# Seven block products in the down projection of an encoder layer's feed-forward part

## The chip, the cores and the metric

One core of one Trainium2 chip runs one launch of the kernel. The time is device microseconds. TensorE (PE) multiplies and writes to PSUM banks of 128 x 512 fp32; VectorE (DVE), ScalarE (ACT) and GpSimd (POOL) work on tiles; SyncE (SP) issues the loads, in order.

## What is computed

One layer of an encoder over 256 rows of width 2048, all in fp32:

```python
h = x + rms_norm(mixed, g_mix_post)          # mixed: attention and recurrence, through w_out
fn = rms_norm(h, g_ffn_pre)
ff = (silu(fn @ w_ffn_gate) * (fn @ w_ffn_up)) @ w_ffn_down   # 2048 -> 5632 -> 2048
h = h + rms_norm(ff, g_ffn_post)
gate = sigmoid(rms_norm(h, g_ple_pre) @ w_ple_gate)
ple = p @ w_ple_proj                          # the embedding, 256 -> 2048
h = h + rms_norm(gate * ple, g_ple_post)
```

## The kernel before

**Products.** Rows are two blocks (t) of 128, contraction blocks (k) are of 128, and columns come in chunks (c) of 512. Each fp32 factor is split into a high part that the fast format holds and a low part; a product of blocks is three matmuls (high x high, high x low, low x high; L521 to L523 in a plain product, L530 to L532 in a seven-product unit). A weight tile holds two contraction blocks by 512 columns, 512 KB: SP loads it into `wr` (L432), ACT casts it into `wh` (L457), DVE subtracts to make `wl` (L482). Some buffers are lent from tiles not needed meanwhile (`lent_w`, `lent_r`, `lent_t`).

**Seven products.** In the gate/up stage a `Group` computes two chunks at once (one of gate, one of up). For a pair of contraction blocks, two row blocks and two chunks, a plain unit (`p`) makes 8 block products, 24 matmuls; an `s` unit makes 7 products in Strassen's manner (`seven`), 21 matmuls. An `s` unit needs sums of weight blocks, two more tiles that DVE makes with four 512-wide operations (L502, L506) and that are cast and split as the others, and sums of the left-hand blocks (`act_sums`). It uses eight banks: four `c` sums that every unit adds to, and four `p` sums that `Seven`-type code in `early` combines (one ACT copy, four DVE additions) once the last `s` unit is through; `late` then adds them to the `c` sums. The two rings of four banks swap roles from group to group (`flip`). The kinds of a gate/up group:

```python
FIRST = "ppppspsp"
KINDS = "ppspspsp"
```

**Stages of the feed-forward part.** The 5632 columns are 11 gate/up groups, in parts of 4, 4 and 3. After each part the down projection adds that part's share: for each of four chunks in turn, `seg` runs 8 (part 2: 6) plain pairs into two banks `acc`, and `down_post` copies them to `mg` on ACT (part 0) or adds them to it on DVE (part 1); in part 2 `sub_post` adds them, squares them on ACT and multiplies by the gain. The last gate/up group of a part is finished inside the down stage: six late operations (L1506, L1513), two transposes of four matmuls (L309), and the split of the result into `mid0h` and `mid0l` (L289, L291).

**Order.** Every engine takes its queue in order. The order across engines is set while the program is written: a planner keeps a clock for each engine, with a cost for each kind of instruction, and picks, of the tasks that are ready, the one that would start first; a task may be given an advance or a delay (`late`).

**The embedding.** Its first half (chunks 0 and 1, tile `ple0`, 1 MB) is made ahead of the feed-forward part and kept on the chip until the last stage; the second half is made after the down projection from the same split `pTh`, `pTl` of p. As the gate/up stage begins, `lend_h` saves h to DRAM (L1328) and lends its space to weight tiles; `give_back` reloads it in part 2 (L1348).

Of the kernel before, what the change touches and what calls it, by code (L numbers as in the profile page):

```python
# [61 lines left out]
LANDED = 2.5  # L62
FIRST = "ppppspsp"
# [164 lines left out]
def layer(ctx: ExitStack, tc: tile.TileContext, a: dict, out: bass.AP):  # L228
# [140 lines left out]
    class Group:  # L369


        def __init__(self, w, n0, lhs, ks, kinds, post):
            self.lhs, self.post, self.banks, self.i0 = lhs, post, {}, len(tiles)
            self.early = Event()
            self.units = list(zip(ks, kinds))
            self.early = Event()
            for (k, _), kind in self.units:
                i = len(tiles)
                tiles.extend((w[c], k, n0[c]) for c in range(2))
                by_dma.update({"d": (i, i + 1), "e": (i + 1,), "c": (i,)}.get(kind, ()))  # L380
                if kind == "s":
                    singles[i + 1] = 1
                    for n in range(2):
                        sums[i + 2 + n] = (i, n)
                        tiles.append(None)
            segs.append(self)
# [174 lines left out]
    def run_group(g, flip):  # L561
        rings = ("sm", "acc") if flip else ("acc", "sm")
# [596 lines left out]
    def open_p2():  # L1159
# [7 lines left out]
        t2["ple", 0] = rs.tile([P, NT, DA], F32, name="ple0")  # L1167
# [4 lines left out]
        t2["pTh"] = rs.tile([P, 2, S], F32R, name="pTh")  # L1172
        t2["pTl"] = rs.tile([P, 2, S], F32R, name="pTl")
        t2["pw"] = rs.tile([P, NT, N], F32, tag="mid", name="pw", bufs=2)[:, 0, :]
        t2["pw"] = t2["pw"].rearrange("p (k s) -> p k s", k=2)
# [10 lines left out]
    pT = Act(2)  # L1186
# [10 lines left out]
    def load_p2():  # L1197
        yield from load_gain("g_mix_post")
        done(ev_gain["mix"])
        yield dma(256)  # L1200
        here = Event()
        nc.sync.dma_start(t2["pw"], a["pT"].rearrange("(k p) s -> p k s", p=P))
        done(here)
# [3 lines left out]
        done(ev_h)  # L1207
        yield here
        yield from split(t2["pTh"], t2["pTl"], t2["pw"], 2 * S)
        pT.blocks(t2["pTh"], t2["pTl"], 0, 2)  # L1210
        pT.pair(0)

    class Sub:
# [10 lines left out]
        def chunk(self, c, ch, add=False):  # L1224
# [29 lines left out]
            if early:  # L1254
                yield ev_gain[self.name]
                for t in range(NT):
# [3 lines left out]
                    )  # L1260
            done(self.chunks[c])
# [11 lines left out]
    def next_norm(sub, nxt, rstd, ev_rstd, g_next):  # L1273
# [21 lines left out]
        for c in range(4):  # L1295
            if c > 1:
                yield nxt.ev[4 * c - 8]
            for b in range(2):
# [7 lines left out]
                plan.add(transpose_h(4 * c + 2 * b, hi, lo, nxt, sub.gname), plan.now)  # L1306
# [31 lines left out]
    def lend_gain():  # L1338
        t = t2["pool"].tile([P, 2, 2, N], F32, tag="gain", name="lent_t")
        lend("ts", [t[:, n, :, :] for n in range(2)])  # L1340

# [83 lines left out]
    def ple_post(c):  # L1425
        def post(ch):
# [3 lines left out]
            release(ch)  # L1430
        return post

    def embedding(c):
        seg(Chunk(ple_post(c)), "w_ple_proj", c * N, pT, [(0, 0)])
# [6 lines left out]
    def sub_post(sub, c, add=False, after=None):  # L1441
        def post(ch):
            if c == 3:
                plan.add(after(), plan.now)
# [3 lines left out]
    def after_mix():  # L1448
# [5 lines left out]
        Chunk(sub_post(mix, c, after=after_mix), None if c else open_p2) for c in range(4)  # L1454
# [16 lines left out]
    class Gated:  # L1471


        def __init__(self, mid, kk0):
            self.mid, self.kk0 = mid, kk0
# [20 lines left out]

        def late(self, g):
# [4 lines left out]
            for t, n, x in (  # L1502
                (0, "c11", e[:, 0, :]), (1, "c21", e[:, 1, :]), (0, "c12", u[0]), (1, "c22", u[1]),
            ):
# [3 lines left out]
                if n[2] == "1":  # L1508
# [29 lines left out]
    class Mid(Act):  # L1538
        def __init__(self, name):
            super().__init__()  # L1540
            self.name, self.halves = name, {}

        def tiles(self, i):
            if i not in self.halves:
                t = (big(2 * i, f"{self.name}h{i}"), big(2 * i + 1, f"{self.name}l{i}"))
                self.halves[i] = t
                self.blocks(*t, 8 * i, 8)
            return self.halves[i]

    def down_post(part, c):  # L1550
        def post(ch):
            sl = slice(c * N, (c + 1) * N)
            mg = t2["mg"]
            for t in range(NT):
                if part == 0:
                    yield act(N)
                    nc.scalar.copy(mg[:, t, sl], ch.accs[t])
                else:
                    yield dve(N)
                    nc.vector.tensor_tensor(  # L1560
                        out=mg[:, t, sl], in0=ch.accs[t], in1=mg[:, t, sl], op=ALU.add
                    )
            release(ch)
        return post
# [7 lines left out]
    for part, (f0, f1) in enumerate(parts):  # L1572
# [5 lines left out]
        for c in range(4):  # L1578
            last = part == len(parts) - 1
            post = sub_post(ffn, c, True, after_ffn) if last else down_post(part, c)  # L1580
            seg(Chunk(post), "w_ffn_down", c * N, mid,
                [(f0 * 4 + k, k) for k in range(0, (f1 - f0) * 4, 2)],
                after=(lambda: load_sqrt()) if last and c == 3 else None)
# [183 lines left out]
```

## Time and profile before

| | |
|---|---|
| median of 3 runs | 1179.17 us (1179.09 to 1180.56) |
| profiled execution: time, span | 1181.19 us, 1179.4 us |
| granted TensorE clock | 0.997 |
| busy: PE, DVE, ACT | 1159.9, 878.8, 686.9 us |
| moved by DMA | 236.43 MB, 200 GB/s |

Times in the profile count from the span's first instruction. A row of a group or of the timeline names line, engine, operation, output<-inputs and shapes; in square brackets stands the idle time of the engine ahead of it and what ended it. The gate/up stage runs from about 361 us, with the down stages of parts 0, 1 and 2 at 534.7 to 622.6, 791.4 to 879.3 and 1006.4 to 1072.6 us.

### The profile page before, as it was taken

To read this page: it belongs to the slowest core of one execution; us is meant where nothing else is said; L and a number is where in the kernel's file an instruction comes from. 1 tells how busy PE (TensorE), PEld (TensorE's weight loads), DVE (VectorE), ACT (ScalarE), POOL (GpSimd) and SP (SyncE) were. 2 spreads that over 40 slices of the span, in tenths; PEclk is the share of its full clock that TensorE was granted. 3 is DMA by queue.
4 is the path that set the end of the run, shared out by engine and by line. 5 is a ranking of instruction groups with operands and counts; after the bars stand their busy time and mean duration, and the time that the engine had idled before them with its cause. 6 is when DMAs were issued, how large, how long until landed. Compare 5 with 4: busy or idle time off the path is not lost.

```text
span 1179.4 us, 14527 instructions
## 1 busy us (share of the span) xinstructions
PE 1159.9 (98%) x5292; PEld 959.8 (81%) x5292; DVE 878.8 (75%) x1118; ACT 686.9 (58%) x925; POOL 1.6 (0%) x13
## 2 busy tenths in 40 slices
PE   7999999999999999999999999999999999999996
PEld 5888888888888888888888888888888888888885
DVE  5567868778649898897456899895466988757663
ACT  6687777766548565465445556554335556456652
POOL 0000000000000000000000000000000000000000
PEclk9999999999999999999999999999999999999998
DMA  8855566545963755677665575576656557764851
GB/s 302 286 164 189 168 194 194 163 159 168 327 214 114 289 197 179 213 232 247 191 195 164 164 235 175 177 255 213 195 163 195 167 178 249 270 190 146 259 167 71
DMA packets 69783, 236.43 MB, mean 200 GB/s; under 512 B 7504, under 2 KB 13520, under 8 KB 68560
## 3 DMA queue, kind: packets, MB, share of 16 engines
q1 hardware_dynamic: 69568, 235.44, 61.7%
q8 instruction: 41, 0.67, 0.2%
q14 instruction: 30, 0.25, 0.1%
q10 hardware_dynamic: 144, 0.08, 0.0%
HBM read 231.29 MB, written 4.19 MB: 200 GB/s over the span
## 4 chain that ended last, share of the span: by engine, by line
PE 87%; DVE 6%; DMA 3%; ACT 2%; issue 1%; SPq 1%; DVEq 0%; ACTq 0%
PE acc L523 17%; PE acc L522 17%; PE acc L521 17%; PE c L521 7%; PE c L522 7%; PE c L523 7%; DVE wl L482 2%; PE p L531 2%; PE p L532 2%; PE p L530 2%; PE c L530 2%; PE c L532 2%; PE c L531 2%; PE tr L309 2%; DMA av<-in_w_rg_i 1%
## 5 line engine op out<-in xcount | busy, mean ns | idle before, releaser
L482 DVE TENSOR_TENSOR wl<-wr,wh 128x1024 fp32r<-128x1024 f32 (+1 forms) x322 | 375.9, 1182 | 145.0 <-ACT wh L457 144.3
L457 ACT CAST wh<-wr 128x1024 fp32r<-128x1024 f32 (+1 forms) x322 | 323.5, 1020 | 221.8 <-PE acc L523 135.3
L521 PE MATMUL c<-wh,hT_mix_hi 128*128 128x512 f32 x400 | 157.3, 393 | 0.0
L523 PE MATMUL c<-wh,hT_mix_lo 128*128 128x512 f32 x400 | 155.8, 390 | 0.0
L522 PE MATMUL c<-wl,hT_mix_hi 128*128 128x512 f32 x400 | 155.8, 389 | 0.0
L521 PE MATMUL acc<-wh,hT_hi 128*128 128x512 f32 x320 | 129.0, 403 | 6.5 <-ACT wh L457 6.4
L522 PE MATMUL acc<-wl,hT_hi 128*128 128x512 f32 x320 | 126.7, 396 | 1.7 <-DVE wl L482 1.7
L523 PE MATMUL acc<-wh,hT_lo 128*128 128x512 f32 x320 | 126.6, 396 | 0.0
L457 ACT CAST wh<-lent_t 128x1024 fp32r<-128x1024 f32 x56 | 58.6, 1052 | 56.6 <-DVE lent_t L506 36.7
L523 PEld LDWEIGHTS c<-wh,hT_mix_lo 128*128 128x128 f32 x400 | 75.1, 188 | 16.0 <-DVE hT_mix_lo L297 0.2
L521 PEld LDWEIGHTS c<-wh,hT_mix_hi 128*128 128x128 f32 x400 | 75.1, 188 | 15.1
L522 PEld LDWEIGHTS c<-wl,hT_mix_hi 128*128 128x128 f32 x400 | 75.2, 188 | 15.0
L482 DVE TENSOR_TENSOR wl<-lent_r,wh 128x1024 fp32r<-128x1024 f32 (+1 forms) x58 | 64.4, 1118 | 22.2 <-ACT wh L457 22.1
L457 ACT CAST wh<-lent_r 128x1024 fp32r<-128x1024 f32 (+1 forms) x58 | 55.4, 969 | 41.7 <-PE acc L523 25.0
L521 PEld LDWEIGHTS acc<-wh,hT_hi 128*128 128x128 f32 x320 | 61.2, 191 | 18.9 <-ACT wh L457 7.2
L482 DVE TENSOR_TENSOR wl<-lent_t,wh 128x1024 fp32r<-128x1024 f32 x56 | 66.9, 1218 | 10.6 <-ACT wh L457 10.5
L522 PEld LDWEIGHTS acc<-wl,hT_hi 128*128 128x128 f32 x320 | 61.1, 191 | 14.6 <-DVE wl L482 2.9
L523 PEld LDWEIGHTS acc<-wh,hT_lo 128*128 128x128 f32 x320 | 61.1, 191 | 13.0
L521 PE MATMUL acc<-wh,hT_ffn_hi 128*128 128x512 f32 x112 | 44.0, 393 | 0.0
L521 PE MATMUL acc<-wh,mid0h 128*128 128x512 f32 x112 | 43.8, 391 | 0.0
L521 PE MATMUL acc<-wh,mid1h 128*128 128x512 f32 x112 | 43.8, 391 | 0.0
L523 PE MATMUL acc<-wh,hT_ffn_lo 128*128 128x512 f32 x112 | 43.7, 390 | 0.0
(324 smaller groups left out, 2239.6 us busy)
## 6 DMA issues: line engine op xcount, KB each, us to landing
wr<-in_w_in SPq DMA_DIRECT2D x79, 512.0 KB, 4.3
wr<-in_w_ffn_down SPq DMA_DIRECT2D x68, 512.0 KB, 4.3
wr<-in_w_ffn_gate SPq DMA_DIRECT2D x60, 512.0 KB, 4.2
wr<-in_w_ffn_up SPq DMA_DIRECT2D x60, 512.0 KB, 4.6
wr<-in_w_out SPq DMA_DIRECT2D x32, 512.0 KB, 4.5
wr<-in_w_ple_gate SPq DMA_DIRECT2D x32, 512.0 KB, 4.4
lent_r<-in_w_ffn_gate SPq DMA_DIRECT2D x28, 512.0 KB, 3.9
lent_r<-in_w_ffn_up SPq DMA_DIRECT2D x28, 512.0 KB, 4.4
```

The lines of the kernel that those rows point to most:

```text
L309: nc.tensor.transpose(tr[:, b, t * P : (t + 1) * P], src, ident)
L457: nc.scalar.copy(his[i][:, j, :], raws[i][:, j, :])
L482: nc.vector.tensor_tensor(out=los[i][:, j, :], in0=raws[i][:, j, :], in1=f32(his[i][:, j, :]), op=ALU.subtract,)
L521: nc.tensor.matmul(accs[t], hi[:, sl], wh[:, j, :], start=st, stop=False)
L522: nc.tensor.matmul(accs[t], hi[:, sl], wl[:, j, :], start=False, stop=False)
L523: nc.tensor.matmul(accs[t], lo[:, sl], wh[:, j, :], start=False, stop=sp)
L530: nc.tensor.matmul(o, lh, wh, start=start, stop=False)
L531: nc.tensor.matmul(o, lh, wl, start=False, stop=False)
L532: nc.tensor.matmul(o, ll, wh, start=False, stop=stop)
```

## The change

The down projection works in groups of two chunks with `s` units: in parts 0 and 1 two groups with two and three of them; in part 2 one group with one, and chunks 2 and 3 plain as before. `Down` takes the place of `down_post`: its `early` is that of the gate/up groups (now in a base class `Seven`), its `late` adds the combined sums to `mg`. `mid_sums` makes the block sums of `mid` in two tiles, for which it uses the space of `ple0` and of the split p. So the first half of the embedding is written to DRAM once made (`kept_ple`) and read back in part 2, when p is loaded and split a second time (`ple_back`). The squares, the transposes and the final additions of the last chunk of a sub-layer get an advance of 2 us in the planner (`URGENT`).

```diff
+DOWN = {
+    4: ("p2 p6 p10 p8 s0 p12 s4 p14", "p2 p6 s0 p10 s4 p12 s8 p14"),
+    3: ("p2 p6 p10 s0 p4 p8", ""),
+}
+URGENT = -2.0
...
     def run_group(g, flip):
+        if g.after:
+            g.after()
...
-                plan.add(self.squares(c, t, src, squared[t]), plan.now)
+                plan.add(self.squares(c, t, src, squared[t]), plan.now, URGENT if c == 3 else 0.0)
...
-                plan.add(transpose_h(4 * c + 2 * b, hi, lo, nxt, sub.gname), plan.now)
+                plan.add(transpose_h(4 * c + 2 * b, hi, lo, nxt, sub.gname), plan.now, URGENT)
...
+    def ple_back():
+        yield from load_pT(pTs[1])
+        t2["ple", 0] = t2["pool"].tile([P, NT, DA], F32, tag="ple0", name="ple0")
+        yield dma(1024)
+        nc.sync.dma_start(t2["ple", 0], t2["kept", "ple"])
+
+    def mid_sums(mid, ks):
+        rs = t2["pool"]
+        a_ = rs.tile([P, 2, 2, 4, P], F32R, tag="ple0", name="sums_a")
+        b_ = rs.tile([P, 2, 4, P], F32R, tag="pT", name="sums_b")
...
+        for k, (hi, lo) in zip(ks, at_):
+            mid.sums[k] = hi, lo
+            yield mid.ev[k]
+            yield mid.ev[k + 1]
+            yield dve(2 * S, take="uv")
+            v = at.tile([P, 2, NT, P], F32, tag="at0_hi", name="v")
+            nc.vector.tensor_tensor(
+                out=v.rearrange("p k t m -> p k (t m)"), in0=f32(mid.pair_of(k, 0)),
+                in1=f32(mid.pair_of(k, 1)), op=ALU.add,
+            )
+            yield from act_sums(mid, k, v)
...
             release(ch)
+            if c == 1:
+                t2["kept", "ple"] = kept.tile([P, NT, DA], F32, name="kept_ple")
+                yield dma(1024)
+                nc.sync.dma_start(t2["kept", "ple"], t2["ple", 0])
...
+    class Down(Seven):
...
+        def late(self, g):
+            yield g.early
+            mg, c0 = t2["mg"], self.c0
+            for t, c, n, x in self.parts():
+                to = mg[:, t, (c0 + c) * N : (c0 + c + 1) * N]
+                if self.part:
+                    yield dve(N)
+                    nc.vector.tensor_tensor(out=to, in0=x, in1=to, op=ALU.add)
+                    x = to
+                yield dve(N)
+                nc.vector.tensor_tensor(out=to, in0=g.banks[n], in1=x, op=ALU.add)
+                g.give(n)
...
-        for c in range(4):
-            last = part == len(parts) - 1
-            post = sub_post(ffn, c, True, after_ffn) if last else down_post(part, c)
-            seg(Chunk(post), "w_ffn_down", c * N, mid,
+        for n in range(1 if last else 2):
+            Group(("w_ffn_down",) * 2, (2 * n * N, (2 * n + 1) * N), mid,
+                  [(f0 * 4 + k, k) for _, k in units[n]], [kind for kind, _ in units[n]],
+                  Down(part, 2 * n, ffn if last else None),
+                  after=(lambda mid=mid, ks=summed: plan.add(
+                      mid_sums(mid, ks), plan.clk["pe"], LATE_SUMS)) if n == 0 else None)
+        for c in range(2, 4) if last else ():
...
```

PE, the pair of blocks 0 and 1 of `mid0` in the down stage of part 0. Before, it stands once for each chunk; the first block of one chunk:

```order
L521 MATMUL acc_4646<-wh,mid0h_3661 128x512
L522 MATMUL acc_4646<-wl,mid0h_3661 128x512
L523 MATMUL acc_4646<-wh,mid0l_3662 128x512
L521 MATMUL acc_4647<-wh,mid0h_3661 128x512
L522 MATMUL acc_4647<-wl,mid0h_3661 128x512
L523 MATMUL acc_4647<-wh,mid0l_3662 128x512
```

With the change it is the unit `s0` of the first group, for both chunks; its first four products (`p` and `c` are banks, `sums_a` the sums of mid's blocks):

```order
L537 MATMUL p_4822<-lent_w,mid0h_3662 128x512
L538 MATMUL p_4822<-lent_w,mid0h_3662 128x512
L539 MATMUL p_4822<-lent_w,mid0l_3663 128x512
L537 MATMUL c_4649<-lent_w,mid0h_3662 128x512
L538 MATMUL c_4649<-lent_w,mid0h_3662 128x512
L539 MATMUL c_4649<-lent_w,mid0l_3663 128x512
L537 MATMUL c_4672<-wh,sums_a 128x512
L538 MATMUL c_4672<-wl,sums_a 128x512
L539 MATMUL c_4672<-wh,sums_a 128x512
L537 MATMUL p_4842<-wh,sums_a 128x512
L538 MATMUL p_4842<-wl,sums_a 128x512
L539 MATMUL p_4842<-wh,sums_a 128x512
```

Each chunk had four such triples for each of the two row blocks' pairs, 24 matmuls for two chunks; now there are seven triples, 21.

DVE, entry of the same stage, before (`mid` and `u` are the last gate/up group's tiles, the L1506 and L1513 rows its late operations; `wl` tiles are weights for the down projection):

```order
L482 TENSOR_TENSOR wl<-lent_r,wh 128x1024 x2
L1506 TENSOR_TENSOR mid<-c_4299,mid 128x512
L1506 TENSOR_TENSOR mid<-c_4300,mid 128x512
L1506 TENSOR_TENSOR u_hi<-c_4319,u_hi 128x512
L1506 TENSOR_TENSOR u_lo<-c_4320,u_lo 128x512
L1513 SCALAR_TENSOR_TENSOR mid<-u_hi,rstd_f,mid 128x512
L1513 SCALAR_TENSOR_TENSOR mid<-u_lo,rstd_f,mid 128x512
L482 TENSOR_TENSOR wl<-wr,wh 128x1024 x2
L291 TENSOR_TENSOR mid0l_4342<-tr,mid0h_4341 128x512
L482 TENSOR_TENSOR wl<-wr,wh 128x1024 x2
L291 TENSOR_TENSOR mid0l_4342<-tr,mid0h_4341 128x512
L482 TENSOR_TENSOR lent_w<-lent_r,lent_w 128x1024
```

With the change, from the first row behind those late operations (`v` and `s` build the sums of mid's blocks, the rows into `sums_a` are their low parts):

```order
L1390 TENSOR_TENSOR v<-mid0h_3662,mid0l_3663 128x512
L1466 TENSOR_TENSOR s<-v 128x128
L1466 TENSOR_TENSOR s<-s,v 128x128
L1466 TENSOR_TENSOR s<-v 128x128
L1466 TENSOR_TENSOR s<-v,s 128x128
L297 TENSOR_TENSOR mid0l_4343<-tr,mid0h_4342 128x512
L297 TENSOR_TENSOR sums_a<-s,sums_a 128x512
L489 TENSOR_TENSOR wl<-wr,wh 128x1024
L1390 TENSOR_TENSOR v<-mid0h_3662,mid0l_3663 128x512
L297 TENSOR_TENSOR mid0l_4343<-tr,mid0h_4342 128x512
L1466 TENSOR_TENSOR s<-v 128x128
L489 TENSOR_TENSOR wl<-wr,wh 128x1024
```

Where low parts of weights followed the late operations, two of the three sums of mid's blocks now stand among them.

DVE, a little later with the change, where the tiles of the unit `s0` are made (`lent_t` takes the sums of weight blocks):

```order
L489 TENSOR_TENSOR lent_w<-lent_r,lent_w 128x1024
L297 TENSOR_TENSOR sums_b<-s,sums_b 128x512
L489 TENSOR_TENSOR wl<-lent_r,wh 128x512
L509 TENSOR_TENSOR lent_t<-lent_r 128x512
L513 TENSOR_TENSOR lent_t<-lent_r 128x512
L509 TENSOR_TENSOR lent_t<-lent_r,lent_t 128x512
L513 TENSOR_TENSOR lent_t<-lent_r,lent_t 128x512
L489 TENSOR_TENSOR wl<-lent_t,wh 128x1024 x2
L509 TENSOR_TENSOR lent_t<-wr 128x512
L489 TENSOR_TENSOR wl<-wr,wh 128x1024 x2
```

Before, this stretch held low parts alone; the four sums of weights and the third sum of mid's blocks are new there.

SP, as the gate/up stage begins, before (`wr` and `lent_r` take weights, `kept0` and `kept1` the two halves of h):

```order
L432 DMA wr_3143<-in_w_ffn_gate 128x1024
L432 DMA wr_3313<-in_w_ffn_up 128x1024
L432 DMA wr_3341<-in_w_ffn_gate 128x1024
L432 DMA wr_3356<-in_w_ffn_up 128x1024
L1328 DMA kept0_3387<-h0_2694 128x2048
L1328 DMA kept1_3388<-h1_2695 128x2048
L432 DMA lent_r_3415<-in_w_ffn_gate 128x1024
```

With the change, from one load earlier:

```order
L439 DMA wr_3142<-in_w_ffn_gate 128x1024
L1488 DMA kept_ple_3204<-ple0_2696 128x2048
L439 DMA wr_3319<-in_w_ffn_up 128x1024
L439 DMA wr_3344<-in_w_ffn_gate 128x1024
L439 DMA wr_3359<-in_w_ffn_up 128x1024
L1358 DMA kept0_3388<-h0_2694 128x2048
L1358 DMA kept1_3389<-h1_2695 128x2048
L439 DMA lent_r_3416<-in_w_ffn_gate 128x1024
```

The write of the first half of the embedding stands three weight loads ahead of the saving of h.

More of the change, by code (lines that the diff above doesn't have):

```diff
@@ L1199, in load_p2, with more_h @@
         done(ev_gain["mix"])
[L1200 to L1203, printed above, removed]
+        yield from load_pT(pTs[0], more_h())
+    def more_h():
         for t in range(NT):
@@ L1207, in load_p2, with load_pT @@
         done(ev_h)
+    def load_pT(pT, then=()):
+        yield dma(256, take="mid")
+        pw = t2["pool"].tile([P, NT, N], F32, tag="mid", name="pw", bufs=2)[:, 0, :]
+        pw = pw.rearrange("p (k s) -> p k s", k=2)
+        here = Event()
+        nc.sync.dma_start(pw, a["pT"].rearrange("(k p) s -> p k s", p=P))
+        done(here)
+        yield from then
         yield here
-        yield from split(t2["pTh"], t2["pTl"], t2["pw"], 2 * S)
-        pT.blocks(t2["pTh"], t2["pTl"], 0, 2)
+        t = t2["pool"].tile([P, 2, 2, S], F32R, tag="pT", name="pT")
+        yield from split(t[:, 0, :, :], t[:, 1, :, :], pw, 2 * S)
+        plan.free["mid"].append(plan.now)
+        pT.blocks(t[:, 0, :, :], t[:, 1, :, :], 0, 2)
         pT.pair(0)
@@ L1443, in post @@
             if c == 3:
-                plan.add(after(), plan.now)
+                plan.add(after(), plan.now, URGENT)
             yield from sub.chunk(c, ch, add)
@@ L1453, in layer @@
     ch = [
-        Chunk(sub_post(mix, c, after=after_mix), None if c else open_p2) for c in range(4)
+        Chunk(sub_post(mix, c, after=after_mix), None if c else open_p2, URGENT if c == 3 else 0.0)
+        for c in range(4)
     ]
@@ L1507, in late @@
                 g.give(n)
-                if n[2] == "1":
+                if not c:
                     plan.add(self.silu(t, gated[t]), plan.now)
```

100 lines of the change are left out of this document (61 added, 39 removed).

## The prediction

> **What bounds the kernel now.** I read the busy shares first, then the chain that ended last, then the stages.
>
> ```profile
> PE 1159.9 (98%) x5292; PEld 959.8 (81%) x5292; DVE 878.8 (75%) x1118; ACT 686.9 (58%) x925; POOL 1.6 (0%) x13
> PE 87%; DVE 6%; DMA 3%; ACT 2%; issue 1%; SPq 1%; DVEq 0%; ACTq 0%
> ```
>
> TensorE carries 87% of the chain. A busy share could still hide gaps, so the stages come next (start:end, length, then busy time with the number of instructions of PE, PEld, DVE, ACT, POOL, the granted clock, the DMA share, GB/s).
>
> ```profile
> 0.00:350.00 350.00, 341.32 (x1617) 283.77 (x1618) 248.32 (x357) 240.24 (x362) 1.60 (x13) 1.00 0.65 211
> 350.00:400.00 50.00, 49.75 (x232) 40.30 (x231) 40.88 (x77) 34.17 (x68) 0.00 (x0) 1.00 0.54 183
> 492.00:534.70 42.70, 42.70 (x194) 35.35 (x193) 38.88 (x47) 24.76 (x28) 0.00 (x0) 1.00 0.60 200
> 534.70:622.60 87.90, 87.90 (x393) 72.82 (x392) 48.36 (x47) 39.36 (x43) 0.00 (x0) 1.00 0.68 213
> 791.40:879.30 87.90, 87.90 (x393) 72.80 (x392) 50.59 (x53) 35.73 (x36) 0.00 (x0) 1.00 0.66 203
> 1006.40:1072.60 66.20, 66.18 (x296) 54.84 (x297) 41.83 (x45) 32.56 (x42) 0.00 (x0) 1.00 0.71 228
> 1072.60:1090.00 17.40, 17.30 (x93) 14.22 (x92) 16.24 (x39) 14.11 (x30) 0.00 (x0) 1.00 0.27 101
> 1150.00:1180.00 30.00, 19.44 (x86) 15.77 (x84) 10.09 (x18) 8.38 (x16) 0.00 (x0) 0.87 0.18 70
> ```
>
> The fourth, fifth and sixth rows are the three down stages: PE without a gap, DVE at 55%, 58% and 63%. The third is a gate/up group, which already works with seven products: PE without a gap too, though DVE is at 91%. So in the down stages matmuls are the time, and DVE has room there. PE idles 8.7 us before 350 (mostly the first loads) and 10.6 us after 1150 (the last chunk's tail); the change touches neither.
>
> **The matmuls taken out.** The pitch of a 128x512 matmul, from the first and last of 30 plain ones and of 20 of a gate/up group's last seven products and what follows (start, duration):
>
> ```profile
> 534.67 0.39 PE L521 MATMUL acc<-lent_w,mid0h 128*128 128x512 f32 x1
> 541.24 0.40 PE L523 MATMUL acc<-wh,mid0l 128*128 128x512 f32 x1
> 524.69 0.39 PE L531 MATMUL p<-wl,hT_mix_hi 128*128 128x512 f32 x1
> 529.00 0.39 PE L532 MATMUL c<-wh,hT_mix_lo 128*128 128x512 f32 x1
> 541.48 0.60 PE L309 MATMUL tr<-ident,mid 128*128 128x128 f32 x4
> 1006.42 0.47 PE L521 MATMUL acc<-wh,mid2h 128*128 128x512 f32 x1 [0.52 <-DVE mid L1506]
> ```
>
> 6.57 / 29 = 0.2266 and 4.31 / 19 = 0.2268: I take 0.2267 us in both forms, and the listed 0.39 us is pipelined. A pair of row blocks over two chunks takes 24 matmuls, in the new form 7 products of three, 21. Units of kind s: two and three in part 0, the same in part 1, one in part 2: 11. So 33 matmuls go, 33 x 0.2267 = **7.48 us**. PE's order in the built programs has 33 rows less, and no transposes are added.
> The Trainium skill ("TensorE: Matmul & The Clock Gate", section "Back-to-back issue gap") gives some 131 ns as the sustained spacing at 512 columns; by that figure the term would be 4.3 us. The two pitches just worked out do not agree with it, and they decide.
>
> The last row shows 0.52 us of PE idle ahead of part 2's down stage: the first chunk took banks of the ring whose sums the gate/up group's late additions (L1506) had not yet read. The new down group is one more in the alternation of rings, so its c sums take the ring that the early additions emptied. I count this **0.5 us** as gone; its bounds are 0 and 0.52.
>
> **What is added, mostly on DVE.** Durations overlap on DVE, so I use start-to-start pitches; this is part 0's entry.
>
> ```profile
> 528.82 0.69 DVE L1484 TENSOR_TENSOR mid<-p,mid 128x512 f32<-128x512 f32 x1 [0.86 <-PE p L532]
> 529.54 0.69 DVE L1488 TENSOR_TENSOR u_hi<-p,mid 128x512 f32<-128x512 f32 x1
> 531.60 2.35 DVE L482 TENSOR_TENSOR wl<-lent_r,wh 128x1024 fp32r<-128x1024 f32 x2
> 533.87 1.28 DVE L1506 TENSOR_TENSOR mid<-c,mid 128x512 f32<-128x512 f32 x2
> 535.07 0.68 DVE L1506 TENSOR_TENSOR u_hi<-c,u_hi 128x512 f32<-128x512 f32 x1
> 537.91 2.35 DVE L482 TENSOR_TENSOR wl<-wr,wh 128x1024 fp32r<-128x1024 f32 x2
> 542.73 0.69 DVE L291 TENSOR_TENSOR mid0l<-tr,mid0h 128x512 fp32r<-128x512 f32 x1 [2.47 <-ACT mid0h L289]
> 543.34 2.35 DVE L482 TENSOR_TENSOR wl<-wr,wh 128x1024 fp32r<-128x1024 f32 x2
> 545.92 0.69 DVE L291 TENSOR_TENSOR mid0l<-tr,mid0h 128x512 fp32r<-128x512 f32 x1 [0.24 <-ACT mid0h L289]
> 374.32 0.49 DVE s L1412 x2
> 540.35 1.05 ACT L457 CAST wh<-lent_r 128x1024 fp32r<-128x1024 f32 x1 [1.67 <-PE acc L523]
> ```
>
> So 1.14 us for 1024 elements (2.27 for the two at 531.60), 0.60 for 512, 0.72 where each waits for the one before (528.82 to 529.54), 0.245 for 128.
> A plain pair costs DVE 2 x 1.14 = 2.28 us; an s unit 3 x 1.14 + 0.60 for the low parts and 4 x 0.60 for the two weight sums, 6.42 us, or 4.1 more. Over 11 units: 46 us. The sums of mid's blocks cost 0.60 + 4 x 0.245 + 0.60 = 2.2 us each, seven of them: 15 us. Each group has four early additions (2.9 us) and four late (2.4 us), eight in parts 1 and 2, in place of ACT copies or four additions. ACT gains 1.5 casts a unit, 11 x 1.5 x 1.05 = 17 us; in part 0 it now works 39.4 of 87.9 us, so that is free. Per group, with what falls in from the one before:
> - first group of parts 0 and 1: 6 x 2.28 + 2 x 6.42 + 2.9 + the gate/up group's late six (3.7) and two low parts (1.2) + 6.5 of sums = 40.8 us, while PE needs 186 x 0.2267 + 0.92 = 43.1: 95%;
> - second group: 5 x 2.28 + 3 x 6.42 + 2.9 + 2.4 (part 1: 4.8) = 36.0 to 38.4 us against 183 x 0.2267 = 41.5: 87% to 92%.
> A gate/up group by the same count is 5 x 2.28 + 3 x 6.42 + 2.9 + 3.7 + 1.2 = 38.5 against 42.4, 91%, and the trace has 91% there with no gap. DVE thus has the throughput; only the first group is above what the trace has shown to be free.
>
> **The entry, step by step.** I walk part 0's first group along its DVE order with the clock of the trace. The late six end at about 537.9 as now. The first v and s take 1.6 us, to 539.5; then mid0l waits for the transposes, which stand after 30 matmuls in both orders (541.48), so it starts at 542.73 as now. mid0l and the first sums' low part, 1.2, then the fifth tile's low part, 1.14, end at 545.1. PE asks for it at 534.67 + 49 x 0.2267 + 0.92 (the transposes) = 546.7, since the second matmul of a tile is the first to read its low part: 1.6 us to spare. From the second mid0l (done 546.5) to the first weight-sum tile of s0 stand 12.5 us of rows (two sums, five low parts, four weight-sum operations, that tile): 559.0, and PE asks at 534.67 + 106 x 0.2267 + 0.92 = 559.6. The next plain tile, behind the second sum tile: about 562.0, asked at 562.3. The margins are 1.6, 0.6 and 0.3 us. A hand-over costs 0.24 us where the trace shows one (545.92), and the walk leaves some out, so I book 0.3 us at each of the three entries, **0.9 us**; 0 is the lower bound (a gate/up group pays nothing at 91%), and the upper is the 2.47 us wait of the 542.73 row falling at all three, 7.4 us.
>
> **The first half of the embedding** is saved by one 1 MB write, queued on SP between two weight loads.
>
> ```profile
> 358.93 0.33 SPq L432 DMA_DIRECT2D wr<-in_w_ffn_gate  x1
> 374.15 0.33 SPq L432 DMA_DIRECT2D wr<-in_w_ffn_up  x1
> 378.73 0.91 SPq L1328 DMA_DIRECT2D kept<-h  x2
> 388.82 0.33 SPq L432 DMA_DIRECT2D lent_r<-in_w_ffn_gate  x1
> DMA to landing us min/median/max: 6.8/8.3/9.5
> 362.68 0.60 ACT L1429 COPY ple<-acc 128x512 f32<-128x512 f32 x1
> 366.01 0.47 PE L521 MATMUL c<-wh,hT_mix_hi 128*128 128x512 f32 x1
> 399.10 0.50 PE p L531
> ```
>
> SP has nothing to issue between 358.93 and 374.15. The last copy of the embedding moves behind five evacuations in a row, by some 1.0 us, to about 364.3, still ahead of the 366.01 matmul that wants its bank; the write then lands by 364.3 + 9.5 = 373.8, before the saving of h at 378.73. Price 0. If that cover failed, what is late is h's saving, the load at 388.82 behind it and the matmul at 399.10, which the chain reaches with no slack: up to 8.3 us. The return (1.25 MB) is queued behind eight weight loads of part 2, where the DMA share is 0.71; its readers (the second half of the embedding and the gates) come over 20 us later: 0. The second split of pT is one cast and one subtraction, 1.2 us, ahead of a tile that by the same kind of walk has about 4 us to spare: 0. The earlier turn of the last chunk's squares and transposes could at most win the gaps at 350 to 400 and 1072 to 1090, 0.35 us, or lose as much: 0.
>
> **Sum:** -7.48 - 0.52 + 0.9 = **-7.1 us**. The profiled execution took 1181.19 us (span 1179.4), 2.0 above the median 1179.17 of the runs; 1181.19 - 7.1 = 1174.1 in its terms, and 1172.1 as a median.
>
> **Rivals.**
> - *The entries cost more.* ACT takes its queue in order, and in part 2 stands so:
>
> ```profile
> 1011.69 1.05 ACT L457 CAST wh<-wr 128x1024 fp32r<-128x1024 f32 x1 [3.47 <-DMA wr<-in_w_ffn_down]
> 1012.64 0.58 ACT L289 CAST mid2h<-tr 128x512 fp32r<-128x512 f32 x1
> 13.04 0.43 PE acc L523
> 18.16 0.40 PE acc L523
> ```
>
>  There a cast that waited for its load held back mid2h behind it. Now the third pair of part 2 needs that very evacuation, 48 matmuls in, with about half a microsecond to spare; and in parts 0 and 1 the casts of the weight sums wait behind the casts of mid's sums, whose input DVE makes late. At 1 to 2.5 us for each entry in place of 0.3: -8.0 + 3 to 7.5, time 1174.2 to 1176.8 for the lower part of it. Against it: PE's gapless gate/up stages.
> - *Nothing is left.* The same at its bound of 7.4 us, or the save uncovered at 8.3: within 1176.8 to 1181.5.
> - *Slower.* One mechanism: the sums of mid's blocks hold ACT until the third is made, the weight casts behind it start late, and PE waits over 3.5 us at both three-sum entries, long enough for its clock to fall. The last two rows above are a cold start: 0.43 us a matmul from 13.04 to 18.16, 5 us that yield 2.7 us of work. Two waits of 4 us and two cold spells of 2.4 us, with 0.9 elsewhere, are 13.7: 1179.2 - 8.0 + 13.7 = 1184.9. It decides once the entries lose 8 us together. Against it: margins are short, but positive. The Trainium skill ("TensorE: Matmul & The Clock Gate", section "HAM oscillation — how this bites in real kernels") says that idle gaps of more than about 3.4 us halve the clock; the trace has the slow start, but no such gap in mid-kernel.
> - *It doesn't do what it says:* excluded, since the 33 matmuls are gone from the built order.
>
> **How the numbers follow.** Forecast 0.71, dearer entries 0.16, nothing left 0.08, slower 0.05. A change below 0.2% (2.4 us) can't be told from none here, so faster means below 1176.8: 0.71 + 0.16 = 0.87; same 0.08; slower 0.05. The range goes from no loss at all with the 0.35 us won (1179.2 - 8.35 = 1170.8, less 0.2 for scatter) to 1176.2, near the end of the dearer entries; about 0.15 is left out.
>
> **What would show it.** PE with 33 fewer 128x512 matmuls and a pitch still near 0.227; down stages of about 84.5, 84.5 and 65.5 us with under 0.5 us of idle each; DVE near 90% in them; the 0.52 us before part 2 gone; the matmul at 399.10 unmoved. I am wrong if PE waits for wl, wh or mid's low parts in the first 28 us of a down stage, or if the pitch grows while DVE and ACT are busier.

## The result, and the profile after

| | before | after |
|---|---|---|
| median of 4 runs | 1179.43 us | 1173.51 us (1172.38 to 1173.71) |
| ratio | | 0.9946, 95% interval 0.9929 to 0.9963 |
| profiled execution: time, span | 1181.19, 1179.4 us | 1173.45, 1171.7 us |

The change makes the kernel 5.9 us faster; I had forecast 7.1. By the page of the changed kernel PE is busy for 98% of the span as before, with 33 instructions fewer; DVE has gone from 75% to 82%. In the chain that ended last PE has gone from 87% to 82%, and DMA has doubled its share to 6%.

```profile
PE 1150.5 (98%) x5259; PEld 951.6 (81%) x5259; DVE 961.3 (82%) x1267; ACT 701.9 (60%) x952; POOL 1.6 (0%) x13
PE 82%; DVE 6%; DMA 6%; ACT 3%; issue 1%; SPq 1%; DVEq 0%; ACTq 0%
```

The stages of the changed kernel, from the first matmul of one to the first of the next: the three down stages are the first, second and fourth row, part 2's gate/up stage the third, and the last row runs from the second half of the embedding to the end (columns as in the stage rows above).

```profile
533.02:617.63 84.61, 84.61 (x378) 70.05 (x377) 77.38 (x101) 43.51 (x50) 0.00 (x0) 1.00 0.62 204
786.39:870.98 84.59, 84.59 (x379) 70.05 (x377) 79.09 (x105) 43.43 (x50) 0.00 (x0) 1.00 0.58 188
870.98:997.31 126.33, 126.33 (x566) 104.64 (x565) 115.97 (x139) 68.58 (x77) 0.00 (x0) 1.00 0.60 198
997.31:1062.86 65.55, 65.55 (x295) 54.28 (x293) 53.39 (x65) 35.91 (x48) 0.00 (x0) 1.00 0.75 259
1062.86:1171.70 108.84, 97.79 (x441) 79.54 (x439) 67.49 (x97) 61.36 (x104) 0.00 (x0) 0.97 0.47 157
```

PE has no gap in the first four, though DVE works 91% and 93% of the two long down stages (first and second row). The same cuts for the kernel before, with my terms:

| stretch | before | after | measured | forecast |
|---|---|---|---|---|
| start to gate/up | 361.64 | 360.01 | -1.63 | 0 |
| gate/up, parts 0 and 1 | 173.03, 168.76 | 173.01, 168.76 | -0.02 | 0 |
| down, parts 0 and 1 | 87.98, 87.99 | 84.61, 84.59 | -6.77 | -6.80 |
| gate/up, part 2 | 127.02 | 126.33 | -0.69 | -0.52 |
| down, part 2 | 66.31 | 65.55 | -0.76 | -0.68 |
| entries of the three | | | 0 | +0.9 |
| second half of the embedding to the end | 106.67 | 108.84 | +2.17 | 0 |

The start is not the change's: over all profiles of this study, whatever the kernel, it took 359.6 to 362.9 us, and the first profile of before was 1.8 us above the median in the table. Without the start the sum is -6.1, which fits the medians. So the forecast gain is there to a quarter of a microsecond, the entries cost nothing that shows, and **2.2 us are given back in a place to which I had given no price: the last stretch**. Since the down stages and the gate/up stages behind them repeat to about 0.1 us from run to run, the experiments are read by the lengths of stages; the medians, from several chips and with the start in them, stand beside.

**The exit of part 2's group.** What DVE, ACT and SP did there in the changed kernel (timelines: start, duration, engine, line, in brackets the idle time ahead and what ended it):

```profile
1029.62 1.42 SPq L1218 DMA_DIRECT2D pw<-in_pT  x1
1032.72 1.06 ACT L464 CAST wh<-wr 128x1024 fp32r<-128x1024 f32 x1 [2.51 <-DMA wr<-in_w_ffn_down]
1035.17 1.05 ACT L464 CAST wh<-wr 128x1024 fp32r<-128x1024 f32 x1 [0.16 <-DMA wr<-in_w_ffn_down]
1036.13 0.61 ACT L295 CAST pT<-pw 128x512 fp32r<-128x512 f32 x1
1033.31 0.68 DVE L1634 TENSOR_TENSOR mg<-u_lo,mg 128x512 f32<-128x512 f32 x1
1036.78 0.69 DVE L297 TENSOR_TENSOR pT<-pw,pT 128x512 fp32r<-128x512 f32 x1 [2.78 <-ACT pT L295]
1037.98 1.22 DVE L489 TENSOR_TENSOR wl<-wr,wh 128x1024 fp32r<-128x1024 f32 x1
1039.26 6.14 SPq L439 DMA_DIRECT2D wr<-in_w_ffn_down  x4
1062.31 1.05 ACT L464 CAST wh<-wr 128x1024 fp32r<-128x1024 f32 x1 [1.49 <-DMA wr<-in_w_ple_gate]
1063.39 1.23 DVE L489 TENSOR_TENSOR wl<-wr,wh 128x1024 fp32r<-128x1024 f32 x1 [1.31 <-ACT wh L464]
1064.53 1.28 DVE L1251 TENSOR_TENSOR mg<-acc,mg 128x512 f32<-128x512 f32 x2
1068.16 2.46 DVE L1332 SCALAR_TENSOR_TENSOR h<-mg,ro_ffn,h 128x256 f32<-128x256 f32 x6
1070.54 1.22 DVE L489 TENSOR_TENSOR wl<-wr,wh 128x1024 fp32r<-128x1024 f32 x1
```

And PE:

```profile
1068.70 2.52 PE L315 MATMUL tr<-ident,h 128*128 128x128 f32 x12 [0.24 <-DVE h L1332]
1072.61 0.50 PE L530 MATMUL acc<-wh,hT_ffn_lo 128*128 128x512 f32 x1 [0.92 <-DVE hT_ffn_lo L303]
```

The same place before (ACT's last cast ahead of the additions, the last additions, the twelve transposes):

```profile
1070.21 1.05 ACT L457 CAST wh<-wr 128x1024 fp32r<-128x1024 f32 x1 [1.67 <-PE acc L523]
1072.44 1.28 DVE L1236 TENSOR_TENSOR mg<-acc,mg 128x512 f32<-128x512 f32 x2
1078.18 1.47 PE L309 MATMUL tr<-ident,h 128*128 128x128 f32 x12
```

The second split of p stands in DVE's queue ahead of the low parts of four weights. DVE waits 2.78 us for ACT's cast of p, and on ACT that cast stands behind the casts of three of these weights (1032.72 to 1035.17), which come as their loads land. It begins without idle time behind the third. The load of p itself, issued at 1029.62 behind those of the weights, took 6.1 us and had landed 0.4 us before; by these rows a quicker load would not have moved the cast. So the two engines hold p at different places of the weight stream. Only the first low part behind p's split (1037.98) gives its weight buffer back to SP, whose next load goes out at 1039.26. What lead the stream of weights still had is then gone: ACT's casts of the gate weights wait for their loads, and 25 us later the last chunk's additions stand behind a low part that is late (1063.39), and start 1.67 us after the last product (first embedding matmul at 1062.86; before, 0.29 us ahead of it, at 1072.73). So h is late: twelve transposes take 2.52 us instead of 1.47 in before. Then one more low part (1070.54) stands between h's rows, and PE waits 0.92 us for hT's low part. That reading gives two causes, a late stream and an order; the experiments part them.

### The profile page after: what moved, and what is told of

Its sections match the earlier page's. It is cut to its first block, busy times and chain, and to the rows that moved or that the text cites. A ratio compares the mean times of both kernels' runs of the same rounds, so it can differ in the third digit from the quotient of the medians.

```text
span 1171.7 us, 14652 instructions
## 1 busy us (share of the span) xinstructions
PE 1150.5 (98%) x5259; PEld 951.6 (81%) x5259; DVE 961.3 (82%) x1267; ACT 701.9 (60%) x952; POOL 1.6 (0%) x13
## 4 chain that ended last, share of the span: by engine, by line
PE 82%; DVE 6%; DMA 6%; ACT 3%; issue 1%; SPq 1%; DVEq 0%; ACTq 0%
PE c L528 12%; PE c L530 12%; PE c L529 12%; PE acc L530 9%; PE acc L528 9%; PE acc L529 9%; PE p L538 3%; PE p L539 3%; PE p L537 3%; DVE wl L489 3%; PE c L537 2%; PE c L538 2%; PE c L539 2%; PE tr L315 2%; DMA wr<-in_w_ffn_down 1%; DMA xs<-in_xT 1%
## 5 line engine op out<-in xcount | busy, mean ns | idle before, releaser
L489 DVE TENSOR_TENSOR wl<-wr,wh 128x1024 fp32r<-128x1024 f32 (+1 forms) x311 | 358.4, 1167 | 76.0 <-ACT wh L464 75.1
L464 ACT CAST wh<-wr 128x1024 fp32r<-128x1024 f32 (+1 forms) x311 | 307.8, 1008 | 138.8 <-PE acc L530 46.7
L464 ACT CAST wh<-lent_t 128x1024 fp32r<-128x1024 f32 x75 | 78.7, 1052 | 113.0 <-DVE lent_t L513 105.7
L489 DVE TENSOR_TENSOR wl<-lent_t,wh 128x1024 fp32r<-128x1024 f32 x75 | 89.6, 1218 | 1.3 <-ACT wh L464 1.1
L489 DVE TENSOR_TENSOR wl<-lent_r,wh 128x1024 fp32r<-128x1024 f32 (+1 forms) x70 | 76.3, 1102 | 4.7 <-ACT wh L464 4.5
L464 ACT CAST wh<-lent_r 128x1024 fp32r<-128x1024 f32 (+1 forms) x70 | 65.1, 957 | 23.9 <-PE c L530 15.2
L529 PE MATMUL acc<-wl,hT_ffn_hi 128*128 128x512 f32 x112 | 43.6, 389 | 0.0
L1616 ACT ACTIVATE mid<-mid,rstd_f 128x512 f32<-128x512 f32 x22 | 14.7, 716 | 28.8 <-DVE mid L1589 28.8
```

The costliest lines, as they stand in the source:

```text
L464: nc.scalar.copy(his[i][:, j, :], raws[i][:, j, :])
L489: nc.vector.tensor_tensor(out=los[i][:, j, :], in0=raws[i][:, j, :], in1=f32(his[i][:, j, :]), op=ALU.subtract,)
L529: nc.tensor.matmul(accs[t], hi[:, sl], wl[:, j, :], start=False, stop=False)
L1616: nc.scalar.activation(self.e[:, t, :], self.e[:, t, :], AF.Silu, scale=rstd_f[:, t : t + 1])
```

## The experiments

The last stretch took 106.67 us in the profile of before. "Lateness" is the start of the last additions less that of the first embedding matmul behind them: -0.29 before, +1.67 after.

**1. The reload later.** My first suspect was the reload of the embedding, 1 MB between weight loads.

```diff
     def ple_back():
         yield from load_pT(pTs[1])
+
+    def ple_reload():
         t2["ple", 0] = t2["pool"].tile([P, NT, DA], F32, tag="ple0", name="ple0")
...
-    embedding(2)
+    embedding(2, lambda: plan.add(ple_reload(), plan.clk["pe"]))
```

> The 1 MB that brings the first half of the embedding back is issued behind the first eight gate weights of the last stage instead of ahead of the last four down weights; nothing else moves. In the changed kernel the stretch from the second half of the embedding to the end takes 108.8 us, 2.2 more than before. Theory A (the return lies in the way of the weight loads, ACT's casts wait for them, a low part of a weight behind such a cast holds back the last chunk's additions on DVE): ACT's waits for gate weights between 1055 and 1063 us shrink, the last additions start 0.5 to 1.9 us sooner after the last product, the stretch takes 106.9 to 108.0, the time is 1171.5 to 1172.7. Rival B (the advances given in the planner put a weight's low part ahead of the transposes' rows on DVE, loads are not the cause): the stretch stays at 108.6 to 109.0 and the time at 1173.5.

The stretch took 108.68 us, lateness +1.53, the wait on hT's low part 0.92 again, median 1175.25. The reload is not the cause; theory A fell in this form.

**2. No advance.**

```diff
-URGENT = -2.0
+URGENT = 0.0
```

> The advance of 2 us for the last chunk's squares, transposes and additions is set to zero; all else as in the changed kernel, with the order on the engines as the planner then makes it (the low part of a weight no longer stands between h's rows). Theory A (late loads delay the last chunk's additions): the last additions still start about 1.9 us after the last product, only the wait of 0.9 us for a low part of the transposed h goes, and the squares may come later: 107.9 to 109.5 us from the second half of the embedding on, time 1172.6 to 1174.2. Rival B (the order is the cause): the stretch returns to 106.7 to 107.2 us, time 1171.4 to 1171.9.

```profile
1040.21 0.69 DVE L297 TENSOR_TENSOR pT<-pw,pT 128x512 fp32r<-128x512 f32 x1 [2.01 <-ACT pT L295]
1066.89 1.28 DVE L1251 TENSOR_TENSOR mg<-acc,mg 128x512 f32<-128x512 f32 x2
1070.13 3.26 DVE L1332 SCALAR_TENSOR_TENSOR h<-mg,ro_ffn,h 128x256 f32<-128x256 f32 x8
1073.30 0.87 DVE L303 SCALAR_TENSOR_TENSOR hT_ffn_lo<-tr,vec,hT_ffn_hi 128x256 fp32r<-128x256 f32 x2
```

The stretch was 106.51 us, median 1174.71. Eight rows of h now stand together, the low parts of hT right behind them. So the order is one cause. But DVE waited only 2.0 us for p here and lateness was +0.50, so the run does not say what the order does with a stream as late as in the first profile. By the medians of one chip it is 0.5 us faster than run 1, not 2.2: in its profile the stretch is 2.2 us shorter, but the start 1.0 and the first gate/up stage 0.4 us longer.

**3. Part 2 plain.**

```diff
-    3: ("p2 p6 p10 s0 p4 p8", ""),
+    3: ("p2 p6 p10 p0 p4 p8", ""),
...
-        for n in range(1 if last else 2):
+        for n in range(0 if last else 2):
...
-        for c in range(2, 4) if last else ():
+        for c in range(4) if last else ():
```

> Part 2's down projection is left as it was before (four chunks in turn, plain products); parts 0 and 1 and the way of the embedding to memory and back as in the changed kernel. Matmuls: 3 more, +0.68 us. Forecast of the ring: the idle of 0.52 us ahead of part 2's down stage comes back, since the gate/up group's late additions again hold the banks that the first chunk takes; if the ring was not the reason it stays away. Theory A for the last stretch (108.8 us in the changed kernel): the reload still stands there but the gain's load moves out of the stage and the weights' buffers come free sooner, so part of the 2.2 us goes: 107.0 to 108.5. Time 1173.5 + 0.68 + 0.52 - 0.3 to 1.8 = 1172.9 to 1174.4. Rival B (order alone): stretch 108.6 to 109.0, time 1174.5 to 1174.9.

```profile
1038.45 0.69 DVE L297 TENSOR_TENSOR pT<-pw,pT 128x512 fp32r<-128x512 f32 x1 [1.72 <-ACT pT L295]
1064.59 1.28 DVE L1251 TENSOR_TENSOR mg<-acc,mg 128x512 f32<-128x512 f32 x2
1070.60 1.22 DVE L489 TENSOR_TENSOR wl<-wr,wh 128x1024 fp32r<-128x1024 f32 x1
```

Stretch 106.82, lateness -0.29, median 1173.42; part 2's stage 66.31, as before. The bad order is there (1070.60), and costs PE 0.39 us instead of 0.92. DVE waits 1.72 us for p (here ACT's cast of it did wait for the load, 1.58 us), but the additions are not late: from 1046 us on ACT's casts waited for PE, not for loads. With the group and the early split the lateness goes with DVE's wait: -0.29 at 0.59 us (run 9), +0.50 at 2.01 (run 2), +1.5 to +2.3 at 2.6 to 3.2 us (the changed kernel twice, runs 1 and 4). So I take it that both must come together, a lead already used up by the group and the wait for p; a wait of 2.8 us without a group was not tried.
The 0.52 us ahead of part 2's stage did not come back (gate/up 126.37). My reason for it, one more group in the alternation of rings, does not hold; the next rows of before show a likelier one: the early additions stood behind a weight whose cast had waited for its load.

```profile
998.32 1.05 ACT L457 CAST wh<-wr 128x1024 fp32r<-128x1024 f32 x1 [1.49 <-DMA wr<-in_w_ffn_down]
999.40 1.23 DVE L482 TENSOR_TENSOR wl<-wr,wh 128x1024 fp32r<-128x1024 f32 x1 [1.31 <-ACT wh L457]
1000.54 0.68 DVE L1484 TENSOR_TENSOR mid<-p,mid 128x512 f32<-128x512 f32 x1
```

In this run the same addition waited for PE's last seven-product matmul (1.15 us), not for a weight. What in the planner's order or in the loads moved it was not tried.

**4. A third unit in the first groups.**

```diff
-    4: ("p2 p6 p10 p8 s0 p12 s4 p14", ...
+    4: ("p2 p6 p10 s0 p12 s4 s8 p14", ...
```

> The first group of parts 0 and 1 gets a third unit of seven products, on sums that are made in any case: 6 matmuls fewer, -1.36 us. By the count of start-to-start pitches DVE then has 44.9 us of work in the 42.4 us of such a group, 106%. If DVE's order and throughput set the bound there as the count says, PE waits about 2 to 3 us in each of the two groups or at their ends, and the time is 1176 to 1178. If the count is too high by a tenth, or the surplus falls into the second group, which has room, PE does not wait and the time is 1172.1.

Down stages 87.05 and 86.06 us, where matmuls alone would be 84.6 - 0.68 = 83.9: 3.1 and 2.1 us of waiting, of which these rows name 1.8 in the first; the waits of its first unit of seven products stand behind them. Median 1179.95, ratio to before 0.9988 (0.9978 to 0.9998); the last stretch, 109.44 us, is late here too.

```profile
PE p L538 <- DVE wl L489: 1.1, 2, 0.8
PE p L537 <- ACT wh L464: 0.7, 1, 0.7
557.32 0.50 PE L537 MATMUL p<-wh,sums_a 128*128 128x512 f32 x1 [0.66 <-ACT wh L464]
558.58 0.50 PE L538 MATMUL p<-wl,sums_a 128*128 128x512 f32 x1 [0.76 <-DVE wl L489]
557.30 1.23 DVE L489 TENSOR_TENSOR wl<-lent_t,wh 128x1024 fp32r<-128x1024 f32 x1 [0.97 <-ACT wh L464]
```

At the 95% that I counted for two units DVE cost nothing; with three the two stages are only 0.9 and 1.9 us shorter than before, and more than half of their gain is gone. That 106% is the reason is not shown, since the edit also moves `s0` one unit ahead and puts two units of seven products in a row. At `s0` alone PE waits 0.66 and 0.76 us, and there DVE itself waits 0.97 us for a cast of ACT. By my walk of part 0, as an estimate, its first weight-sum tile there would be done at 556.7 (one plain pair's low parts less) and asked for at 554.2 (24 matmuls sooner), so the place alone can make a wait there. A third unit with `s0` left at its place was not tried.

**5. The split of p later.** The direct test of the mechanism at the exit.

```diff
         yield here
+        if pT is pTs[1]:
+            there = Event()
+            there.t = plan.now + 5.0
+            yield there
         t = t2["pool"].tile([P, 2, 2, S], F32R, tag="pT", name="pT")
```

> Only the second split of p moves: the planner is told that p lands 5 us later, so on DVE one weight's low part now stands ahead of p's low part, and two more rows; the reload of the embedding falls behind two more weight loads with it. Theory C (in part 2 DVE waits 2.8 us in its queue for p's cast, whose input has not landed; the low parts behind it give the weight buffers back late, the next loads, casts and low parts run without a lead, and the last chunk's additions wait behind one): DVE's wait of 2.8 us near the end of part 2's group goes, the last additions start at most 0.5 us after the last product, the stretch from the second half of the embedding to the end takes 106.7 to 107.3 us in place of 108.8, the time falls by 1.5 to 2.1 us to 1173.1 to 1173.8 on this chip. Rival D (the lead is lost in any case to the eight additions and four multiplications that end the group): the stretch stays at 108.4 to 108.9, the time at 1175.2.

```profile
1035.10 1.22 DVE L489 TENSOR_TENSOR wl<-wr,wh 128x1024 fp32r<-128x1024 f32 x1
1036.35 2.06 SPq L439 DMA_DIRECT2D wr<-in_w_ffn_down  x2
1039.18 0.68 DVE L297 TENSOR_TENSOR pT<-pw,pT 128x512 fp32r<-128x512 f32 x1
1061.11 1.05 ACT L464 CAST wh<-wr 128x1024 fp32r<-128x1024 f32 x1 [1.48 <-PE acc L530]
1063.33 1.28 DVE L1255 TENSOR_TENSOR mg<-acc,mg 128x512 f32<-128x512 f32 x2
1071.35 0.50 PE L530 MATMUL acc<-wh,hT_ffn_lo 128*128 128x512 f32 x1 [0.33 <-DVE hT_ffn_lo L303]
```

The low part and the load behind it go out ahead of p's split, DVE does not wait for p, the last cast ahead of the additions waits for PE again, and the lateness is -0.30 (additions 1063.33, embedding 1063.63). The stretch took 106.77 us, median 1172.24. That shows the mechanism: with p's split behind two low parts the lateness is gone. The reload of the embedding moved by two weight loads with it, but a later reload alone had changed nothing (run 1). What the order alone leaves is the wait of 0.33 us.

**6. Both.** The later split and `URGENT = 0.0`.

> The later split of p and the planner's advance of 2 us set to zero together. If the stretch's 2.2 us come from late additions and from the weight's low part that the advance puts between h's rows, one of the two is enough to leave little, and both leave nothing: 106.4 to 106.6 us from the second half of the embedding to the end, as with the advance at zero alone (106.5). Counted from the last transposition wait near 193 us to the end, 978.0 to 978.7 us, against 980.3 in the changed kernel. If the two costs add up separately, it is no faster than with the advance at zero alone either way; it is slower than that only if the lead is lost elsewhere.

106.33 us, median 1172.83 (the 0.4 us less in the stretch do not show in the medians); once more, with the changed kernel on the same chip:

> The kernel with the later split of p and no advance once more, for a comparison on the same chip: 106.3 to 106.6 us from the second half of the embedding on; 2.0 to 2.4 us faster than the changed kernel.

> The changed kernel once more, on the same chip as the two above: down stages of 84.6, 84.6 and 65.55 us as in its first profile, the last stretch 108.4 to 108.9 us if its lateness belongs to the program, nearer to 107 if it was a chance of the first chip's loads.

```profile
1063.00:1169.40 106.40, 96.61 (x441) 79.58 (x439) 65.75 (x96) 60.89 (x103) 0.00 (x0) 0.96 0.49 156
```

With both 106.40 us and 1171.33 (1170.90 to 1173.65), ratio to before 0.9919 (0.9906 to 0.9932); the changed kernel 1175.65 (1174.79 to 1176.71), ratio 0.9947 (0.9935 to 0.9959), its stretch 109.43 with DVE's wait for p 2.57 us and lateness +2.28. So the lateness belongs to the program, and a version with both edits is faster than either kernel by more than the intervals.

**7. The write later, and before again.** In all profiles after the first two PE waited 0.2 to 0.8 us near 399 us, the matmul I had named for the write of the embedding. The version with both edits, with the write 40 us later:

```diff
             if c == 1:
+                there = Event()
+                there.t = plan.now + 40.0
+                yield there
                 t2["kept", "ple"] = kept.tile([P, NT, DA], F32, name="kept_ple")
```

> As the run with the later split and no advance, and the write of the first half of the embedding is issued about 40 us later, behind the saving of h and some ten more weight loads; nothing else moves. On this chip the changed kernels waited 0.3 to 0.7 us for a low part at about 400 us, the matmul that I named as the place where the write's price would show. If the write delays h's saving and the load behind it, that wait goes (0 to 0.1 us) and the gate/up stage of part 0 takes 173.0 instead of 173.2 to 173.6. If it is this chip's slower loads, the wait stays and shows in the kernel before as well.

> The kernel before, unchanged, for a profile on the same chip. If the write of the embedding is what delays the matmul at 400 us, there is no wait there and the gate/up stage of part 0 takes 173.0 us; if the loads are slower on this chip, it waits 0.3 to 0.7 us too. The stretch from the second half of the embedding on should take 106.5 to 106.8 us, and the wait ahead of part 2's down stage 0.5 us, as in the first profile.

The row with the later write, then that of before:

```profile
398.68 0.50 PE L538 MATMUL p<-wl,sums_f 128*128 128x512 f32 x1 [0.81 <-DVE wl L489]
399.37 0.50 PE L531 MATMUL p<-wl,sums_f 128*128 128x512 f32 x1 [0.55 <-DVE wl L482]
```

The wait is in before too and does not go with the write. So the write costs nothing that shows; the wait differs from run to run, and the first two profiles happened to have none. In this second profile of before the last stretch is 106.6 us and the lateness -0.29 again, and PE waits 0.63 us ahead of part 2's down stage, as it did in the first (0.52).

**8. Two units in part 2**, on top of both edits.

```diff
-    3: ("p2 p6 p10 s0 p4 p8", ""),
+    3: ("p2 p6 p10 s0 s4 p8", ""),
```

> The later split of p, no advance, and a second unit of seven products in part 2's group: 3 matmuls fewer, -0.68 us, for 4.1 us of weight work and 2.2 us of a further sum on DVE, which works 54 of 66 us there. If DVE's room in the stage is what counts, part 2's down stage takes 64.9 us and the rest stays: 0.7 us faster than with one unit. If it is the lead of the loads (DVE gives back weight buffers later, and the eight rows that end the group come on top), the casts of the gate weights wait for their loads again, the last additions are late and the last stretch grows by 0.5 to 2 us: no gain or a loss.

```profile
PE p L538 <- DVE wl L489: 2.2, 4, 0.8
PE tr L315 <- DVE h L1336: 1.9, 1, 1.9
PE p L537 <- ACT wh L464: 0.6, 2, 0.3
```

Part 2's stage took 69.38 us in place of 64.9, the last stretch 109.14 (lateness +1.69), median 1178.78. The first and third of these rows are 2.8 us within the stage, the second is the last stretch's wait for h: the additions can be late without a wait for p. Over the whole stage DVE works 58 of 69 us: its sum does not decide. The waits within the stage fall on the tiles of weight sums, which DVE handles twice (sum, then low part) and which now stand in two units in a row; another order of the units was not tried.

**9. One unit in each group.**

```diff
-    4: ("p2 p6 p10 p8 s0 p12 s4 p14", "p2 p6 s0 p10 s4 p12 s8 p14"),
+    4: ("p2 p6 p10 p8 s0 p12 p4 p14", "p2 p6 s0 p10 p4 p12 p8 p14"),
```

> One unit of seven products in each of the four groups of parts 0 and 1 in place of two and three: 18 matmuls more than the changed kernel, and the blocks' sums 1 in place of 3 for each part. If the down stages are bound by matmuls alone, each of the two stages grows by 9 x 0.2267 = 2.04 us to 86.65 us. If DVE's work or the hand-overs cost something there, less than that, since a part of it goes with the units.

86.62 and 86.63 us, against 86.65 worked out from the matmuls alone: the other units' DVE work is hidden to the last tenth. The last stretch is 106.84 us here: DVE waited 0.59 us for p, and lateness is -0.29, though part 2's table is the changed kernel's. This is one profile, but a third way to the same conclusion.

## Why the prediction came out as it did

- **Matmuls, -7.48.** The three down stages gave -7.53. Fifteen fewer in each of parts 0 and 1 gave 3.37 and 3.40 us, 0.225 and 0.227 each; as an estimate, the 131 ns of the Trainium skill ("TensorE: Matmul & The Clock Gate", section "Back-to-back issue gap") would have given 1.97, and the trace does not agree with it.
- **0.52 ahead of part 2.** Right in size (-0.69 for the stretch), wrong in its reason: without a group in part 2, in run 3, it was gone as well. What took it away stays open.
- **Entries, +0.9.** Nothing was lost. The walk was better than the price I put on it: it left 0.6 and 0.3 us at the first weight-sum tile and the next plain tile. Measured, the first sum tile (first of the two at 556.22) is done at about 557.4 and read at 557.99, the next plain one (first of the two at 559.23) at about 560.4 and read at 560.72.

```profile
556.22 2.50 DVE L489 TENSOR_TENSOR wl<-lent_t,wh 128x1024 fp32r<-128x1024 f32 x2
559.23 2.35 DVE L489 TENSOR_TENSOR wl<-wr,wh 128x1024 fp32r<-128x1024 f32 x2
557.99 0.39 PE L538 MATMUL p<-wl,sums_a 128*128 128x512 f32 x1
560.72 0.40 PE L529 MATMUL c<-wl,mid0h 128*128 128x512 f32 x1
```

 A booking on top of a walk that already has the hand-overs in its pitches counts them twice.
- **The embedding's way to memory and back, 0.** Right for the write (run 7) and for the reload (run 1).
- **The second split of pT, 0: the step that failed.** I asked only whether its reader, the tile behind it, would be late; it was not. What I left out is that the row stands in DVE's queue ahead of low parts of weights, waits there 2.78 us for a cast that stands on ACT behind three weight casts, and that the rows behind it give buffers back to SP. The price fell 25 us later and on others: moving the split alone brought the stretch from 108.84 to 106.77 us (run 5), and with the order it makes the 2.17 us.
- **The earlier turn of squares and transposes, 0 within 0.35.** Its direct price, 106.77 against 106.33 us (runs 5 and 6), is 0.44 us in the profiles, more than the 0.35 I allowed; with a late stream the row it puts between h's rows costs 0.92.
- **Rivals.** Dearer entries did not come, but one unit further on such waits are there (runs 4 and 8). The slower rival did not come either: between the start and the last matmul PE's longest wait, in any run, was 1.9 us, and the granted clock stayed full. It falls to half only behind the last matmul, which ended at 1162.0 in the changed kernel (the clock is the third figure from the end):

```profile
10.90:1164.60 1153.70, 1146.84 (x5252) 949.49 (x5252) 954.46 (x1254) 695.27 (x940) 0.00 (x0) 1.00 0.61 204
1164.70:1171.70 7.00, 0.00 (x0) 0.00 (x0) 3.06 (x6) 0.45 (x3) 0.00 (x0) 0.50 0.39 150
```

 No run here has a long gap between matmuls, and so none shows there what the Trainium skill ("TensorE: Matmul & The Clock Gate", section "HAM oscillation — how this bites in real kernels") says of idle gaps above 3.4 us.

The median exceeded my forecast by 1.4 us. Of this, 1.0 is the +2.17 that I did not book, less the 0.9 that I did and less 0.2 by which the other stages gained more than forecast; 0.3 is that the median of before stands at 1179.43 in place of 1179.17; the rest is within the scatter of the runs. So a part of the closeness is luck: the booking for the entries, which cost nothing, covered four tenths of the price that I had left out.

## What to carry to other kernels

Price a moved load not only at its reader: look at which engines' queues its conversion stands in, whether both hold it at the same place of the stream, and what the rows behind it release; a wait of 2.8 us on an engine with room took away the lead of the weight stream and came out 25 us later as some 2 us. A walk along the order with start-to-start pitches was good to some 0.3 us here: 95% of DVE by such a count was free. One more unit, at 106% and with a unit moved ahead, cost more than half of the gain of its stages; which of the two did it is open. Where a stage ends on a chain (additions, squares, transposes), follow the change through the exit as carefully as through the entry.

## What was not expected of the hardware

The 256 KB of p took 6.1 us from issue to landing in part 2 and 8.0 us at its first load, while a weight tile of 512 KB took 4.2 to 4.7 us in the median over the kernel. In part 2 it shares this with its neighbours: the three weight loads issued just ahead of p took 5.8 to 5.9 us as well. And the stretch before 360 us, the same program on PE in every kernel, took 359.6 to 362.9 us from profile to profile, more than most of the differences read here.
